# A diffusion-transformer layer with retention and attention: maxima transposed as float16 parts, value sums begun by their own products, one norm moved to VectorE

## The chip, the cores and the metric

The kernel runs on one core of one Trainium2 chip. The core has five engines that run side by side, each with its own queue of instructions in order: TensorE (PE, with its weight loads shown as PEld), VectorE (DVE), ScalarE (ACT), GpSimd (POOL) and SyncE (SP), which here issues the DMA transfers. Engines wait for one another through semaphores. TensorE writes to PSUM, a small memory of eight banks; the other data lies in SBUF. The metric is the device time of one execution in microseconds.

## The reference

One layer for a sequence of 2048 tokens with model width 1024, and a context of 256 tokens. Cut to what matters here:

```python
h = _modulate(_rmsnorm(x, norm1_g), sh1, sc1)
rq, rk, rv, rg, aq, ak, av = jnp.split(h @ w_in, SPLIT_IDX, axis=-1)
...
ret, _, _ = _bidir_retention(rq_h, rk_h, _heads(rv, RET_HEADS), log_gamma, s_f, s_b)
ret = _ret_out(ret, rg, ret_gn_g)
...
s = jnp.einsum('bqkgd,bskd->bkgqs', q, k).astype(jnp.float32) * ATT_SCALE
p = jax.nn.softmax(s, axis=-1).astype(v.dtype)
att = jnp.einsum('bkgqs,bskd->bqkgd', p, v)
...
x = x + g1 * (jnp.concatenate([ret, att], axis=-1) @ w_out)
h2 = _modulate(_rmsnorm(x, norm2_g), sh2, sc2)
x = x + g2 * _sqrelu_mlp(h2, w_ff1, w_ff2)
return _rmsnorm(x, final_norm_g)
```

Attention has 8 query heads of 64 channels on 2 key heads, over 2304 keys (2048 and the 256 of the context). All inputs are float32, and the kernel keeps about that precision by splitting operands into a high part and a remainder and multiplying the parts.

## The kernel before, in words

The kernel runs in three stretches. The first, to about 690 us, projects the input (`products`, L820) and stores queries, keys and the retention's operands to DRAM; its end also takes the row maxima of the first attention group. The second, to about 1640 us, is attention with the retention, the output projection and the second norm woven into it. The third is the feed-forward part.

**Steps and phases.** In the second stretch the order is written by hand. `on(k, phase, fn, ...)` (L988) files a call under a step number and a phase; the loop at L1643 walks the steps, and in each step the phases in the order begin, scores, piece, maximum, early, exp, cast, low, chain, pe, values, late, dma. Each engine executes its instructions in that program order. Besides, there is a list `chain` (L996) of small steps; `link` (L998) issues one of them after each of the phases maximum, low and late, and `settle` (L1002) issues from it until a named result is there.

**Attention.** A `Group` (L141) is one tile of 128 queries and one key head with its four query heads; there are 32 groups, and each takes NK = 18 steps, one for each tile of 128 keys. For group n:

- In steps 18n to 18n+17 `piece` (L160) multiplies queries by keys into a PSUM tile `mp` of 512 columns, and one step later `maximum` (L171, L178) reduces it on VectorE into `nm`. The tag `mp` has two buffers (`psS`, L956); the tile `st` of the scores has two of its own.
- In step 18n+18 `least` (L180) reduces `nm` to the negated row maximum of each head and writes it to columns 64 and 96 of `mt`, a float32 tile that is zero elsewhere but for a constant in column 80 (L974, L976). The two `mt` tiles serve the groups in turn.
- In the next step `turn` (L186) transposes the four heads of `mt` on TensorE into another `mp` tile. `rows` (L191) then copies partitions 64 to 127 of it to the second half of the query tile `qr` as float16, scaled by 1/8192, on ScalarE, and `rows2` (L194, L196), one step later in phase early, overwrites partitions 96 to 127 on VectorE with what float16 rounding left. So the negated maximum enters the scores as two extra rows of the contraction, multiplied by rows of `ks2` that hold 8192.
- From step 18n+22 on, `scores` (L198) makes one score tile per step with two products (L202, L203), `exp` (L205, L208) takes the exponential on ScalarE, `cast` (L210, L212) rounds two key tiles at once to float16 (`phi`), and `low` (L214) subtracts to get the remainder `plo`, on GpSimd for five of nine pairs of key tiles (L219) and on VectorE for the others (L221). Every second step `values` (L223) adds a pair of key tiles to the sums `o0` and `o1`, one PSUM bank each with two heads: for each key tile and head, `plo` times the 65 columns of values and ones (L235), then `phi` times 129 columns, values, ones and the values' remainders (L236). Before a group's first pair, a product of zeros with 258 columns for each bank (L227) clears the sums with the start flag.
- `evacuate`, `invert` and `combine` (L238 to L254) take the sums out and divide by the row sums.

**Output projection and second norm.** `output_tile` (L1248) does this for one tile of 128 tokens every 35 steps: transposes of the retention's and attention's result (L1259), products with `w_out` (L1274 to L1276), the residual sum into `y["x"]` (L1281, tile `xr`), its sum of squares, a store of it to DRAM (`store_x`, L1291), the root (`root`, through `chain`, two instructions on GpSimd, L1009 and L1010), the in-place multiplication by the root (`norm`, L1299, L1301, on GpSimd, three steps after the store is issued), and, for most tiles 3 and 4 steps later, its eight transposes on TensorE (`transpose_x`, L1306, four at a time), followed by `modulate` on VectorE (L1311) and `shift_` on GpSimd (L1316). For the last tile these transposes come from the list `rest`, between the first products of the feed-forward part.

**Feed-forward.** `up_part` (L1522 to L1524), `up_out` (L1542), `up_split` and `make_w2` (through `split16`, L70 and L71), `form_w1` (L1457) and `down` (L1582 to L1585) follow a loop over 32 blocks, with a few of the first block's instructions filed in the last steps of attention.

Of the kernel before, what the change touches and what calls it, by code (L numbers as in the profile page):

```python
# [11 lines left out]
F32 = mybir.dt.float32  # L12
F32R = mybir.dt.float32r
F16 = mybir.dt.float16
BF16 = mybir.dt.bfloat16
I32 = mybir.dt.int32
AF = mybir.ActivationFunctionType
ALU = mybir.AluOpType
AX = mybir.AxisListType
# [3 lines left out]
P = 128  # L23
# [6 lines left out]
NK = NT + NC  # L30
H = 4
CH = 128
HD = 64
# [3 lines left out]
PSHIFT = 8  # L37

ROW = 8192.0
VW = 2 * HD + 1  # L40
# [14 lines left out]
def layer_kernel(ctx: ExitStack, tc: tile.TileContext, a: dict, out: bass.AP):  # L55
    nc = tc.nc
    mm = nc.tensor.matmul

    const = ctx.enter_context(tc.tile_pool(name="const", bufs=1, reuse_waits="tile"))
    dram = ctx.enter_context(tc.tile_pool(name="dram", bufs=1, space=DRAM))  # L60

    ident = const.tile([P, P], F32, name="ident")
    make_identity(nc, ident)

    def split(hi, lo, src, eng=None):
        nc.scalar.activation(hi, src, AF.Copy)
# [74 lines left out]
    class Group:  # L141
# [36 lines left out]
            nc.vector.tensor_reduce(dst, src, axis=AX.X, op=ALU.max, negate=True)  # L178

        def least(self, mt):  # L180
            self.mt = mt
            nm = self.nm.rearrange("p a b c -> p (a b) c")
            for c in (64, 96):
                nc.vector.tensor_reduce(mt[:, :, c], nm, axis=AX.X, op=ALU.min)

        def turn(self):  # L186
            self.m = psS.tile([P, 4, P], F32, name="mp", tag="mp")
            for h in range(4):
                nc.tensor.transpose(self.m[:, h], self.mt[:, h], ident)

        def rows(self):  # L191
            nc.scalar.activation(self.qr[64:, 1], self.m[64:], AF.Copy, scale=1 / ROW)

        def rows2(self):  # L194
            lo = self.qr[96:, 1]
            nc.vector.scalar_tensor_tensor(lo, self.m[96:], 1 / ROW, lo, op0=ALU.mult, op1=ALU.subtract)  # L196

        def scores(self, kt):  # L198
            ps = self.s[kt] = psS.tile([P, 512], F32, name="st", tag="st")
# [23 lines left out]
        def values(self, j):  # L223
            if j == 0:
                self.o = [psV.tile([P, 2, VW], F32, name=f"o{b}", tag=f"o{b}") for b in range(2)]
                for o in self.o:
                    mm(o, zeros, wv[:, 0, :2, :VW], start=True, stop=False)  # L227
            hi, lo = self.hi.pop(j), self.lo.pop(j)
            for i in range(2):
                v = wv[:, self.g, 2 * j + i]  # L230
                for h in range(4):
                    o = self.o[h // 2][:, h % 2]
                    c = slice(h * P, (h + 1) * P)
                    last = 2 * j + i == NK - 1 and h % 2 == 1
                    mm(o[:, : HD + 1], lo[:, i, c], v[:, : HD + 1], start=False, stop=False)  # L235
                    mm(o, hi[:, i, c], v[:, :VW], start=False, stop=last)  # L236

        def evacuate(self):  # L238
            self.so = op.tile([P, 4, VW], F32, name="so", tag="so")
# [727 lines left out]
    nc.vector.tensor_tensor(unit, ident[:, 64:65], ident[:, 96:97], op=ALU.add)  # L967
    nc.vector.tensor_tensor(unit, unit, ident[:, 80:81], op=ALU.add)
    nc.vector.tensor_scalar_mul(unit, unit, ROW)
    zeros = vp.tile([P, P], F16, name="zeros")  # L970
    nc.vector.memset(zeros, 0.0)
    mts = [vp.tile([P, 4, P], F32, name=f"mt{i}") for i in range(2)]
    for mt in mts:
        nc.gpsimd.memset(mt, 0.0)  # L974

        nc.gpsimd.memset(mt[:, :, 80], PSHIFT * math.log(2.0) * HD**0.5)  # L976

    def more_keys(g, i):
        s = slice(i * 768, (i + 1) * 768)
# [8 lines left out]
    def on(k, phase, fn, *args):  # L988
        events.setdefault((k, phase), []).append((fn, args))
# [12 lines left out]
    def settle(what):  # L1002
        while what not in settled:
            link()
# [13 lines left out]
    def attention():  # L1018
        for n, g in enumerate(groups):
            k = NK * n  # L1020
# [5 lines left out]
                    on(k + i + 1, "maximum", g.maximum, i)  # L1026
            else:
                on(k + NK, "begin", g.load)
            on(k + NK, "chain", g.least, mts[n % 2])
            on(k + NK + 1, "piece", g.turn)  # L1030
            on(k + NK + 2, "cast", g.rows)
            on(k + NK + 3, "early", g.rows2)
            k += LAG
            for i in range(NK):
                on(k + i, "scores", g.scores, i)
# [212 lines left out]
    def output_tile(t, k, last):  # L1248
# [49 lines left out]

        def norm():  # L1299
            settle(("f", t))  # L1300
            nc.gpsimd.tensor_scalar(y["x"], y["x"], y["r"], 1.0, op0=ALU.mult, op1=ALU.mult)  # L1301

        def transpose_x(q):
            y["ps"] = bank(1)
# [503 lines left out]
```

## Time and profile before

| | us |
|---|---|
| median of 3 runs | 2947.15 (2943.18 to 2947.17) |
| the profiled execution | 2946.76 |
| its span, first to last instruction | 2945.0 |
| PE busy, share of the span | 2776.2, 94% |
| DVE busy | 2181.6, 74% |
| POOL busy | 1550.2, 53% |
| ACT busy | 1388.0, 47% |

The mean granted TensorE clock was 0.987 of full speed. In the page's groups, a line such as "L178 DVE TENSOR_REDUCE nm<-mp ... x576 | 390.9, 685 | 172.6 <-PE mp L165 143.3" reads: line 178 of the kernel, on VectorE, 576 instructions, 390.9 us busy, 685 ns each on average, 172.6 us of idle time of the engine just before them, 143.3 of it ended by TensorE's product at line 165. "x<-y" names the tile written and the tiles read. In a timeline a row has the start, the duration, the engine and the line, and in brackets the idle time before it with what ended it; instructions of one kind that follow each other are merged (x4). A matmul's recorded duration includes its way through the array, so those of neighbours overlap.

### The profile page before, as it was taken

The numbers are of one execution on the slowest core, as the hardware profiler recorded it, in microseconds if no ns is written. First come the engines' busy times: TensorE is split into PE (matmuls) and PEld (weight loads), VectorE is DVE, ScalarE is ACT, GpSimd is POOL, SyncE is SP. The second block draws the span as 40 slices with busy tenths as digits, with TensorE's granted clock in tenths as the row PEclk, the third lists the DMA queues.
The fourth block names the chain that finished last, engine by engine and source line by source line (L and its number), as shares of the span: only waits on it lengthen the run. The fifth ranks groups of instructions, "written<-read, shape, count | busy, mean of one in ns | idle before, by whom it ended". The sixth has DMA issues, their size and how long they took to land. (4 is left out here: it accounts for less than half of the span.)

```text
span 2945.0 us, 45295 instructions
## 1 busy us (share of the span) xinstructions
PE 2776.2 (94%) x17140; PEld 1648.8 (56%) x17140; DVE 2181.6 (74%) x3330; ACT 1388.0 (47%) x2280; POOL 1550.2 (53%) x1274
## 2 busy tenths in 40 slices
PE   7998898998799999999999899999999899999998
PEld 3777677775566666565666444444444344444443
DVE  5889847647987777777876577778777777777776
ACT  2333323325777777787777433333332333333332
POOL 3536326425876667887656656664443444444332
PEclk9999999999999999999999999999999999999999
DMA  9988843426412123332211723331114511111111
GB/s 300 340 283 280 271 154 107 160 67 201 137 46 81 49 63 121 90 104 85 73 63 51 273 92 101 104 102 60 53 51 154 173 60 47 54 51 51 58 44 58
DMA packets 265305, 346.95 MB, mean 118 GB/s; under 512 B 106231, under 2 KB 163831, under 8 KB 263294
## 3 DMA queue, kind: packets, MB, share of 16 engines
q1 hardware_dynamic: 254806, 336.57, 35.2%
q10 hardware_dynamic: 10280, 7.48, 0.9%
q8 instruction: 135, 2.21, 0.3%
q14 instruction: 84, 0.69, 0.1%
HBM read 272.52 MB, written 71.46 MB: 117 GB/s over the span
## 5 line engine op out<-in xcount | busy, mean ns | idle before, releaser
L178 DVE TENSOR_REDUCE nm<-mp 128x1 f32<-128x512 f32 (+1 forms) x576 | 390.9, 685 | 172.6 <-PE mp L165 143.3
L219 POOL TENSOR_TENSOR plo<-p,phi 128x1024 f16<-128x1024 f32 x160 | 353.7, 2212 | 172.9 <-ACT phi L212 139.6
L208 ACT ACTIVATE p<-st 128x512 f32<-128x512 f32 x576 | 338.1, 597 | 188.5 <-PE st L203 118.7
L1582 PE MATMUL pd<-w2hi,uhi 128*128 128x512 f16 x1024 | 388.0, 379 | 12.9 <-DVE acc L1585 12.6
L1583 PE MATMUL pd<-w2lo,uhi 128*128 128x512 f16 x1024 | 388.0, 379 | 0.6 <-DVE w2lo L71 0.6
L1584 PE MATMUL pd<-w2hi,ulo 128*128 128x512 f16 x1024 | 388.1, 379 | 0.0
L1585 DVE SCALAR_TENSOR_TENSOR acc<-pd,sc,acc 128x512 f32<-128x512 f32 x512 | 366.4, 739 | 5.7 <-PE pd L1584 5.6
L1522 PE MATMUL pu<-hf,w1f 128*128 128x512 f16 x896 | 340.1, 380 | 2.5 <-DVE q L1545 2.0
L1523 PE MATMUL pu<-hf,w1f 128*128 128x512 f16 x896 | 340.0, 379 | 0.0
L1524 PE MATMUL pu<-hf,w1f 128*128 128x512 f16 x896 | 339.8, 379 | 0.0
L824 PE MATMUL pso<-whi,hi_l 128*128 128x512 f32 (+1 forms) x768 | 295.8, 388 | 10.2 <-ACT xs L524 4.3
L212 ACT ACTIVATE phi<-p 128x1024 f16<-128x1024 f32 x288 | 303.8, 1055 | 0.0
L826 PE MATMUL pso<-whi,lo_l 128*128 128x512 f32 (+1 forms) x768 | 293.7, 383 | 4.1 <-DVE lo_l L67 4.1
L825 PE MATMUL pso<-wlo,hi_l 128*128 128x512 f32 (+1 forms) x768 | 292.9, 382 | 0.8 <-DVE wlo L67 0.7
L235 PE MATMUL o<-wv,plo 128*128 128x65 f16 x2304 | 235.9, 193 | 23.9 <-POOL plo L219 17.0
L221 DVE TENSOR_TENSOR plo<-p,phi 128x512 f16<-128x512 f32 x256 | 240.9, 942 | 18.6 <-ACT phi L212 15.7
L236 PE MATMUL o<-wv,phi 128*128 128x129 f16 x2304 | 243.8, 221 | 0.0
L235 PEld LDWEIGHTS <-plo 128*128 128x128 f16 x2304 | 206.7, 98 | 59.8 <-POOL plo L219 25.9
L202 PE MATMUL st<-qr,ks 128*128 128x512 f16 x576 | 220.2, 382 | 12.4 <-ACT p L208 10.4
L1534 POOL TENSOR_TENSOR r<-r 128x512 f32<-128x512 f32 x64 | 66.3, 1039 | 295.2 <-ACT r L1533 295.2
L203 PE MATMUL st<-qr,ks 128*128 128x512 f16 x576 | 220.0, 382 | 0.1
L165 PE MATMUL mp<-ks,qr 128*128 128x512 f16 x512 | 196.7, 384 | 23.0 <-DVE nm L178 22.2
(324 smaller groups left out, 5751.4 us busy)
## 6 DMA issues: line engine op xcount, KB each, us to landing
wm<-in_w_ff SPq DMA_DIRECT2D x64, 512.0 KB, 5.3
w1r<-in_w_ff SPq DMA_DIRECT2D x64, 512.0 KB, 4.6
ws<-in_w_ff SPq DMA_DIRECT2D x124, 256.0 KB, 3.5
wst<-in_w_in SPq DMA_DIRECT2D x60, 512.0 KB, 5.5
wst<-in_w_mod SPq DMA_DIRECT2D x32, 512.0 KB, 6.0
hf<-hp SPq DMA_DIRECT2D x56, 256.0 KB, 3.2
hf<-hf SPq DMA_DIRECT2D x14, 1024.0 KB, 7.1
orv<-rv SPq DMA_DIRECT2D x35, 256.0 KB, 4.0
```

Of the source, the lines that this page charges most:

```text
L178: nc.vector.tensor_reduce(dst, src, axis=AX.X, op=ALU.max, negate=True)
L208: nc.scalar.activation(self.p[kt // 2][:, kt % 2], self.s.pop(kt), AF.Exp, scale=HD**-0.5)
L212: nc.scalar.activation(hi, self.p[j], AF.Copy)
L219: nc.gpsimd.tensor_tensor(lo, p, hi, op=ALU.subtract)
L235: mm(o[:, : HD + 1], lo[:, i, c], v[:, : HD + 1], start=False, stop=False)
L1522: mm(pu[i], whi, hi, start=k == 0, stop=False)
L1523: mm(pu[i], whi, lo, start=False, stop=False)
L1524: mm(pu[i], wlo, hi, start=False, stop=k == 3)
L1582: mm(ps, uh, wh, start=f == 0, stop=False)
L1583: mm(ps, uh, wl, start=False, stop=False)
L1584: mm(ps, ul, wh, start=False, stop=f == NF - 1)
L1585: nc.vector.scalar_tensor_tensor(acc[:, c], ps, sc2, acc[:, c], op0=ALU.mult, op1=ALU.add)
```

## The change

Three edits in the attention stage, one of them in four functions.

The maxima: `least` now appends four small steps to `chain`: one reduction to a 128x4 float32 tile, a multiplication by 1/8192 into column 64 of `mt`, the same minus that column into column 96, and a mark that it is settled. It is filed in phase maximum of the step (begin for the first group) instead of chain. The `mt` tiles are float16, so that column 64 holds the rounded value and column 96 the remainder, and the constant in column 80 is divided by 8192 beforehand. `turn` first settles these steps and uses plain products with a float16 identity, `rows` copies without a scale, and `rows2` is gone.

The values: the products of zeros are gone. In `values` the product with `phi` comes before that with `plo`, and the first one of each bank carries the start flag.

The norm: the in-place multiplication of `y["x"]` by its root runs on VectorE instead of GpSimd, at the same place in the order.

```diff
+    ident16 = const.tile([P, P], F16, name="ident16")
+    nc.vector.tensor_copy(ident16, ident)
...
         def least(self, mt):
+
             self.mt = mt
+            m = sm.tile([P, 4], F32, name="least", tag="least")
             nm = self.nm.rearrange("p a b c -> p (a b) c")
-            for c in (64, 96):
-                nc.vector.tensor_reduce(mt[:, :, c], nm, axis=AX.X, op=ALU.min)
+            chain.append(lambda: nc.vector.tensor_reduce(m, nm, axis=AX.X, op=ALU.min))
+            chain.append(lambda: nc.vector.tensor_scalar_mul(mt[:, :, 64], m, 1 / ROW))
+            chain.append(
+                lambda: nc.vector.scalar_tensor_tensor(
+                    mt[:, :, 96], m, 1 / ROW, mt[:, :, 64], op0=ALU.mult, op1=ALU.subtract
+                )
+            )
+            chain.append(lambda: settled.add(("least", self.n)))
 
         def turn(self):
+            settle(("least", self.n))
             self.m = psS.tile([P, 4, P], F32, name="mp", tag="mp")
             for h in range(4):
-                nc.tensor.transpose(self.m[:, h], self.mt[:, h], ident)
+                mm(self.m[:, h], self.mt[:, h], ident16, start=True, stop=True)
 
         def rows(self):
-            nc.scalar.activation(self.qr[64:, 1], self.m[64:], AF.Copy, scale=1 / ROW)
-
-        def rows2(self):
-            lo = self.qr[96:, 1]
-            nc.vector.scalar_tensor_tensor(lo, self.m[96:], 1 / ROW, lo, op0=ALU.mult, op1=ALU.subtract)
+            nc.scalar.activation(self.qr[64:, 1], self.m[64:], AF.Copy)
...
                 self.o = [psV.tile([P, 2, VW], F32, name=f"o{b}", tag=f"o{b}") for b in range(2)]
-                for o in self.o:
-                    mm(o, zeros, wv[:, 0, :2, :VW], start=True, stop=False)
...
-                    mm(o[:, : HD + 1], lo[:, i, c], v[:, : HD + 1], start=False, stop=False)
-                    mm(o, hi[:, i, c], v[:, :VW], start=False, stop=last)
+
+                    mm(o, hi[:, i, c], v[:, :VW], start=j == i == h % 2 == 0, stop=False)
+                    mm(o[:, : HD + 1], lo[:, i, c], v[:, : HD + 1], start=False, stop=last)
...
-    zeros = vp.tile([P, P], F16, name="zeros")
-    nc.vector.memset(zeros, 0.0)
-    mts = [vp.tile([P, 4, P], F32, name=f"mt{i}") for i in range(2)]
+    mts = [vp.tile([P, 4, P], F16, name=f"mt{i}") for i in range(2)]
     for mt in mts:
         nc.gpsimd.memset(mt, 0.0)
 
-        nc.gpsimd.memset(mt[:, :, 80], PSHIFT * math.log(2.0) * HD**0.5)
+        nc.gpsimd.memset(mt[:, :, 80], PSHIFT * math.log(2.0) * HD**0.5 / ROW)
...
-            on(k + NK, "chain", g.least, mts[n % 2])
+            on(k + NK, "maximum" if n else "begin", g.least, mts[n % 2])
             on(k + NK + 1, "piece", g.turn)
             on(k + NK + 2, "cast", g.rows)
-            on(k + NK + 3, "early", g.rows2)
...
         def norm():
             settle(("f", t))
-            nc.gpsimd.tensor_scalar(y["x"], y["x"], y["r"], 1.0, op0=ALU.mult, op1=ALU.mult)
+            nc.vector.tensor_scalar_mul(y["x"], y["x"], y["r"])
```

## The prediction

> **What bounds the kernel now.** I read the page's strip of 40 slices for the stages, then the table by windows for their balance, then the waits of the stage that changes.
>
> ```profile
> 690.00:820.00 130.00, 105.01 (x1014) 74.14 (x1013) 117.73 (x218) 91.54 (x146) 99.04 (x67) 0.97 0.53 170
> 820.00:1640.00 820.00, 773.84 (x7226) 508.85 (x7224) 630.14 (x1105) 622.20 (x1019) 571.71 (x429) 1.00 0.25 78
> 1640.00:1720.00 80.00, 68.26 (x313) 31.20 (x312) 47.18 (x63) 26.55 (x49) 41.43 (x37) 0.98 0.72 265
> 1720.00:2945.00 1225.00, 1200.78 (x5552) 542.83 (x5549) 910.79 (x1182) 415.68 (x670) 551.49 (x421) 1.00 0.23 75
> ```
>
> Each row of the table by windows gives the stretch, its length, then the busy time of PE, PEld, DVE, ACT and POOL. The change touches attention (690 to 1640 us) and, through the norm, the hand-over to the feed-forward part (1640 to 1720). In the body of attention PE is busy 774 of 820 us, DVE 630, ACT 622, POOL 572: **TensorE sets the pace**, and the others have 20 to 30% in hand. The first 130 us are different: DVE is busy 118 of 130 and PE only 105. After 1720 nothing is changed and PE is busy 98%, so whatever is gained or lost before then arrives at the end unchanged.
>
> What PE waits for in 690 to 1640 (waiter, awaited, us in total, times, longest):
>
> ```profile
> DVE nm L178 <- PE mp L165: 119.2, 158, 2.0
> PEld L235 <- POOL plo L219: 25.9, 25, 3.0
> PE mp L165 <- DVE nm L178: 20.6, 34, 2.0
> PE o L235 <- POOL plo L219: 17.0, 13, 2.5
> PE o L235 <- DVE plo L221: 6.7, 14, 1.0
> PE bank L1306 <- POOL xr L1301: 3.5, 7, 1.1
> ```
>
> DVE waits for PE six times as long as PE for DVE, which fits a stage led by PE with short stalls. The groups that the change edits, over the whole span:
>
> ```profile
> L196 DVE SCALAR_TENSOR_TENSOR qr<-mp,qr 32x512 f16<-32x512 f32 x32 | 22.3, 697 | 4.8 <-ACT qr L192 3.8
> L1301 POOL TENSOR_SCALAR xr<-xr,cy_f 128x1024 f32<-128x1024 f32 x16 | 21.6, 1352 | 8.8 <-DMA x<-xr 8.8
> L227 PE MATMUL o<-wv,zeros 128*128 128x258 f16 x64 | 12.3, 274 | 0.0
> L184 DVE TENSOR_REDUCE mt<-nm 128x4 f32<-128x20 f32 x64 | 7.9, 165 | 0.0
> ```
>
> **1. TensorE work.** A matmul's recorded duration overlaps its neighbours, so I price by start to start, in a group without stalls:
>
> ```profile
> 834.48 0.60 PE L189 MATMUL mp<-ident,mt 128*128 128x128 f32 x4
> 834.92 0.38 PE L165 MATMUL mp<-ks,qr 128*128 128x512 f16 x1
> ...
> 849.60 0.39 PE L227 MATMUL o<-wv,zeros 128*128 128x258 f16 x2
> 849.82 0.19 PE L235 MATMUL o<-wv,plo 128*128 128x65 f16 x1
> 849.86 0.22 PE L236 MATMUL o<-wv,phi 128*128 128x129 f16 x1
> 849.91 0.19 PE L235 MATMUL o<-wv,plo 128*128 128x65 f16 x1
> ```
>
> The two zero products hold PE for 849.82 - 849.60 = 0.22 us per group; 32 groups: **7.0 us** go. Their row shows no idle time before them, so they hid no wait; should plo be late there, the cover of 0.22 us is lost, and the gain is smaller by that much. The four float32 transposes take 834.92 - 834.48 = 0.44 us. Float16 products of 128 columns are not in the trace; the nearest row is the 129-column float16 product, and a pair of 65 and 129 columns takes 0.09 us (849.82 to 849.91), so 128 columns take 128/194 of that, 0.06. Four: 0.24, a gain of 0.20 per group, **6.4 us** over 32. Ends: 0 (they cost what they did) to 7.7 (0.05 each). I take 6.4, since that row has the same type, nearly the same width and a weight load per product.
>
> The Trainium skill, "TensorE: Matmul & The Clock Gate", Back-to-back issue gap, gives about 81 ns per product for sustained pairs of weight load and 128-column matmul; by that the gain would be 32 x (0.44 - 0.32) = 3.8 us, an estimate from that page. The rows here speak against it: 0.09 us holds two such pairs.
>
> **2. High part first.** Each product of 129 columns now precedes the one that waits for plo. In the 27 waits of L235 (13 for POOL, 14 for DVE) PE has 0.06 us to do first: 1.6 us at most, I take **1.5**.
>
> **3. The maxima off VectorE.** The 32 instructions of L196 (22.3 us) go. The two reductions (L184, 0.165 us each) become one and two instructions on 128x4; I price those by L184 too, the nearest row with 128x4 out, so one such instruction more per group, +5.3 us in all. VectorE is relieved of 17.0 us here. ACT's copy (L192) keeps its size. Nothing on PE waits for L196, so its time counts only through what is queued behind it, and through the mp buffer that it holds. That buffer is worth a look:
>
> ```profile
> 742.80 0.25 DVE L184 TENSOR_REDUCE mt<-nm 128x4 f32<-128x20 f32 x2
> 744.08 0.68 DVE L178 TENSOR_REDUCE nm<-mp 128x1 f32<-128x512 f32 x1
> ...
> 743.19 0.63 PE L189 MATMUL mp<-ident,mt 128*128 128x128 f32 x4
> 744.81 0.38 PE L165 MATMUL mp<-ks,qr 128*128 128x512 f16 x1 [0.99 <-DVE nm L178]
> 747.86 0.38 PE L165 MATMUL mp<-ks,qr 128*128 128x512 f16 x1 [1.80 <-DVE nm L178]
> ...
> 744.15 0.59 ACT L192 ACTIVATE qr<-mp 64x512 f16<-64x512 f32 x1
> 749.00 0.70 DVE L196 SCALAR_TENSOR_TENSOR qr<-mp,qr 32x512 f16<-32x512 f32 x1
> ```
>
> Of two mp buffers one holds the transposed maxima from 743.19 until L196 ends at 749.70, and the next group's pieces share the other, each waiting for the reduction of the one before. After the change ACT's copy frees it at 744.74, three microseconds before the piece that waits until 747.86. Whether that piece gets it is decided when tiles are placed, which no row shows: 0 to all of the 20.6 us of that wait. I take **4**, near the low end, because the stalls I read are longest in the first 130 us, where DVE is full and a buffer alone does not help.
>
> The added wait: the transposes now need the third small instruction, issued behind the late phase of the step. Here that phase fills DVE from 743.05 to the next reduction at 744.08, so they could start about 744.2 instead of 743.19, with the next piece queued behind them on PE; but that piece waits for the reduction until 744.81 anyway. Cost 0 to 1.1 us in a group; where the late phase has nothing for DVE, none. I take **+0.5** in all.
>
> **4. The norm.** POOL loses 21.6 us. The seven attention waits of L1306 for it (**3.5 us**) go. POOL's plo tensors are no longer behind it: of 42.9 us (two views of the same stalls) I take **2**, between 0 and 6. VectorE gets 16 instructions, priced by the same shape and operation early in the program (minimum, median, maximum in ns):
>
> ```profile
> L416 DVE TENSOR_SCALAR x_l<-x_l,ry_x x16: 741/748/1230, 27.1 to 334.6; 128x1024 f32<-128x1024 f32 x16
> ```
>
> 16 x 0.75 = 12 us, so that VectorE's sum still falls by 5. They come in lumps, with the next reduction and so a piece on PE behind each. DVE's 158 waits for PE show slack that absorbs a lump within a few steps: I take 0.2 each, **+3**, between 0 and 16 x 1.23 = 20.
>
> **5. The hand-over.** The norm works in place, so it waits for the store of its tile. Twice that store is late, and then VectorE's queue stands, not POOL's:
>
> ```profile
> 1657.36 1.12 POOL L1301 TENSOR_SCALAR xr<-xr,cy_f 128x1024 f32<-128x1024 f32 x1 [3.74 <-DMA x<-xr]
> 1681.33 1.12 POOL L1301 TENSOR_SCALAR xr<-xr,cy_f 128x1024 f32<-128x1024 f32 x1 [5.06 <-DMA x<-xr]
> ...
> 1652.83 0.69 DVE L1266 TENSOR_TENSOR rl<-bank,rh 128x512 f16<-128x512 f32 x1
> 1676.47 0.68 DVE L1545 TENSOR_TENSOR r<-pu,w 128x512 f32<-128x512 f32 x1
> ...
> 1655.80 0.38 PE L1276 MATMUL bank<-wo,rl 128*128 128x512 f16 x1
> 1690.35 0.38 PE L1583 MATMUL pd<-w2lo,uhi 128*128 128x512 f16 x1 [0.61 <-DVE w2lo L71]
> ```
>
> At the first, rl (1652.83) is issued behind the norm and would start at 1657.36 + 0.75 = 1658.1; PE's 1655.80 product then starts near 1658.8, and the transposes, now at 1658.53, about 1.1 us later. At the second, everything of the first feed-forward block from 1676.47 on is behind the norm, so it starts at 1682.1; through r, ACT's relu and the splits, the w2lo that PE awaits at 1690.35 comes about 4 us later. Together **+5**, between +1 and the two waits whole, 8.8.
>
> **Sum.** -7.0 - 6.4 - 1.5 - 4 + 0.5 - 3.5 - 2 + 3 + 5 = -15.9. The profiled execution took 2946.8 us (span 2945.0), the median of the runs is 2947.15, so the sum applies to either: **2931 us**, forecast 2923 to 2940, chance 0.55.
>
> **Rivals.** *More comes free* (0.15): the freed buffer ends most of its stall (12 rather than 4), POOL's relief is worth 4, the norm's lumps and the hand-over cost 2 each: -7.0 - 6.4 - 1.5 - 12 - 3.5 - 4 + 4 = -30, **2917**. For it: DVE's and POOL's totals both fall. Against: the largest of these stalls lie where DVE is full.
>
> *The gain turns into another wait* (0.20): PE arrives earlier at products whose plo or p come no earlier. Half of the 13.4 us is lost, no buffer and no POOL relief is gained: -6.7 - 3.5 + 0.5 + 3 + 5 = -1.7, **2945**. For it: PE's waits for plo. Against: DVE and ACT are 20 to 25% idle.
>
> *The norm holds up VectorE* (0.10): each of 16 lumps reaches PE whole at L416's longest, 1.23 us, and both store waits count in full: 19.7 + 8.8 + 0.5 - 13.4 - 3.5 = +12, **2959**, slower. It decides from (13.4 + 3.5 - 8.8 - 0.5) / 16 = 0.48 us of PE time per norm. For it: L416's 1230 beside its median of 748. Against: in 14 of 16 tiles POOL's norm did not wait for the store. The Trainium skill, "SBUF — State Buffer", Who interferes with whom, has a rule that would bring this about: a VectorE instruction in a two-port mode and GpSimd lock each other out of a shared port for a whole instruction, and a scalar multiply from SBUF to SBUF is of that kind. L416's spread agrees with it; no row shows it at this place.
>
> That float16 transposes cost what float32 ones did would give 2937, inside the forecast.
>
> **Chances.** The measurement of this kernel can tell about 0.2% (6 us) from no change. Faster 0.69, the same 0.20, slower 0.11. The range 2914 to 2948 leaves out the end of the first rival, the upper end of the second, and the third.
>
> **What would show it.** No zero products; L189 float16 with 0.06 us between starts; L196 gone; DVE busy lower by 3 to 7 us, POOL by about 20; no wait of L1306 for POOL; in the hand-over DVE waiting for the store twice, 8 us together. Wrong if PE's waits on DVE or plo in 690 to 1640 grow by over 10 us, or if the stage is not shorter by about 20 us while the stretch 1640 to 1720 is longer by about 5.

## The result and the profile after

| | before | after |
|---|---|---|
| median | 2947.16 us (2943.18 to 2950.87, 4 runs) | 2988.12 us (2987.28 to 2988.95, 4 runs) |
| ratio to before | | 1.0139 [1.0122, 1.0157] |
| span of the profiled execution | 2945.0 us | 2986.7 us |
| mean granted clock | 0.987 | 0.981 |

The change made the kernel 41 us slower; 2931 was predicted, with 2914 to 2948 as its range. In the changed kernel the reduction to `least` is L187, the multiplication L188, the subtraction L190, the float16 transposes L200, the pieces L167, the maxima L180, the value products L241 (`phi`) and L242 (`plo`), VectorE's subtraction L228 and GpSimd's L226, the norm L1304 and its transposes L1309.

First the table by windows of the changed kernel, in the stretches used before (length, busy time of PE, PEld, DVE, ACT and POOL, granted clock, DMA):

```profile
690.00:820.00 130.00, 102.38 (x956) 72.09 (x955) 112.98 (x208) 85.22 (x136) 93.15 (x63) 0.92 0.51 164
820.00:1640.00 820.00, 749.41 (x6911) 487.09 (x6909) 652.32 (x1094) 604.59 (x990) 538.28 (x399) 0.98 0.24 72
1640.00:1720.00 80.00, 64.06 (x452) 36.82 (x450) 35.11 (x52) 32.35 (x60) 43.83 (x40) 0.94 0.62 226
```

In the body PE is busy 749 us where it was 774, and does fewer instructions (6911 for 7226) at a lower granted clock (0.98 for 1.00): it stands more. DVE is busy 652 for 630, though work was taken from it. The last score product of attention starts at 1662.0 us, at 1631.7 before: **30 of the 41 us are lost inside attention**, and 11 more between there and the tenth down product. After that the difference stays at 41.7.

The waits of PE in the changed kernel from 690 to 1670, where its attention ends:

```profile
PE mp L167 <- DVE nm L180: 27.0, 37, 2.5
PE mp L200 <- DVE mt L190: 22.0, 14, 3.5
PE o L242 <- POOL plo L226: 16.1, 15, 2.8
PE o L242 <- DVE plo L228: 8.2, 14, 1.2
```

The second line is new in size: the transposes wait 22 us for `mt`. The wait for the maxima has grown from 20.6 to 27.0 us, and that for `plo` (23.7 then, 24.3 now) has not moved, although the norm is gone from GpSimd's queue.

What VectorE's new instructions took, by their tile (minimum, median, maximum in ns, starts of the first and the last):

```profile
L187 DVE TENSOR_REDUCE least<-nm x32: 159/174/175, 659.4 to 1632.0; 128x4 f32<-128x20 f32 x32
L188 DVE TENSOR_SCALAR mt<-least x32: 161/172/2086, 659.7 to 1632.7; 128x4 f16<-128x4 f32 x32
L190 DVE SCALAR_TENSOR_TENSOR mt<-least,mt x32: 144/177/2092, 659.9 to 1632.9; 128x4 f16<-128x4 f32 x32
L1304 DVE TENSOR_SCALAR xr<-xr,cy_f x16: 752/1760/2616, 876.7 to 1717.9; 128x1024 f32<-128x1024 f32 x16
```

The reduction never exceeds 175 ns. The two others have the same size and nearly the same median, yet some of them last twelve times as long: 9 of the 32 of L188 and 7 of L190 are over 0.47 us. The norm, priced at 0.75 us, has that as its minimum and 1.76 as its median. The timelines of DVE and of POOL at two such places show what they stand for:

```profile
1418.96 0.17 DVE L187 TENSOR_REDUCE least<-nm 128x4 f32<-128x20 f32 x1
1420.32 2.09 DVE L188 TENSOR_SCALAR mt<-least 128x4 f16<-128x4 f32 x1
1422.44 0.18 DVE L190 SCALAR_TENSOR_TENSOR mt<-least,mt 128x4 f16<-128x4 f32 x1
...
876.67 2.62 DVE L1304 TENSOR_SCALAR xr<-xr,cy_f 128x1024 f32<-128x1024 f32 x1
```

```profile
1419.81 2.57 POOL L226 TENSOR_TENSOR plo<-p,phi 128x1024 f16<-128x1024 f32 x1
...
876.16 2.57 POOL L226 TENSOR_TENSOR plo<-p,phi 128x1024 f16<-128x1024 f32 x1
```

L188 writes four numbers per partition and ends at 1422.41, 0.03 us after GpSimd's subtraction (1419.81 + 2.57 = 1422.38), which had begun before it. The norm begins while GpSimd's instruction runs (to 878.73) and needs some 0.6 us after that. **A VectorE instruction of these kinds that begins beside a running GpSimd instruction stands until that one has ended.** The Trainium skill, "SBUF — State Buffer", Who interferes with whom, says that `tensor_scalar` in a two-port mode contends with GpSimd, that a VectorE instruction with two inputs in SBUF contends with a GpSimd instruction that reads SBUF, that whoever issues first holds the shared port and the other blocks, and that `tensor_reduce` on trn2 never contends. The four rows agree: the reduction takes 175 ns at most, the three others up to 2.1 and 2.6 us. In which mode L188 and L1304 run, no row shows.

The trace of before had a row that says the same, which the prediction did not read: VectorE's own subtraction, two inputs in SBUF, as a line of its tile.

```profile
L221 DVE TENSOR_TENSOR plo<-p,phi x256: 673/689/2635, 691.8 to 1635.1; 128x512 f16<-128x512 f32 x128
```

A median of 689 ns beside a maximum of 2635, in the stage that the change touches. In the trace of before, 81 of these 256 instructions take over 0.9 us; each of the 81 begins while a GpSimd instruction runs and ends 0.54 to 0.55 us after it.

The hand-over, in DVE's timeline and then in PE's, of the changed kernel:

```profile
1687.37 0.75 DVE L1304 TENSOR_SCALAR xr<-xr,cy_f 128x1024 f32<-128x1024 f32 x1 [4.31 <-DMA x<-xr]
1688.03 0.68 DVE L1269 TENSOR_TENSOR rl<-bank,rh 128x512 f16<-128x512 f32 x1
...
1717.93 0.75 DVE L1304 TENSOR_SCALAR xr<-xr,cy_f 128x1024 f32<-128x1024 f32 x1 [7.23 <-DMA x<-xr]
```

```profile
1688.77 1.12 PE L1262 MATMUL bank<-ident,ma 128*128 128x128 f32 x4 [5.21 <-DVE rl L1269]
...
1718.74 1.12 PE L1309 MATMUL bank<-ident,xr 128*128 128x128 f32 x4 [4.64 <-DVE xr L1304]
```

VectorE waits for the two late stores (11.5 us together), and PE stands 5.2 us behind `rl`, which is queued behind the first, and 4.6 us for the second norm itself.

### The profile page after: what moved, and what is told of

Same layout as the page of the kernel before. It is cut to its first block, busy times and chain, and to the rows that moved or that the text cites. A ratio compares the mean times of both kernels' runs of the same rounds, so it can differ in the third digit from the quotient of the medians.

```text
span 2986.7 us, 45103 instructions
## 1 busy us (share of the span) xinstructions
PE 2779.3 (93%) x17076; PEld 1644.9 (55%) x17076; DVE 2221.6 (74%) x3346; ACT 1388.8 (46%) x2280; POOL 1531.0 (51%) x1258
## 5 line engine op out<-in xcount | busy, mean ns | idle before, releaser
L180 DVE TENSOR_REDUCE nm<-mp 128x1 f32<-128x512 f32 (+1 forms) x576 | 389.9, 684 | 163.5 <-PE mp L167 138.7
L226 POOL TENSOR_TENSOR plo<-p,phi 128x1024 f16<-128x1024 f32 x160 | 354.9, 2219 | 184.2 <-ACT phi L219 151.6
L1585 PE MATMUL pd<-w2hi,uhi 128*128 128x512 f16 x1024 | 388.0, 379 | 15.3 <-DVE acc L1588 12.4
L228 DVE TENSOR_TENSOR plo<-p,phi 128x512 f16<-128x512 f32 x256 | 254.6, 996 | 22.8 <-ACT phi L219 22.2
L242 PE MATMUL o<-wv,plo 128*128 128x65 f16 x2304 | 237.5, 194 | 24.7 <-POOL plo L226 16.1
L241 PE MATMUL o<-wv,phi 128*128 128x129 f16 x2304 | 248.0, 222 | 0.0
L242 PEld LDWEIGHTS <-plo 128*128 128x128 f16 x2304 | 204.5, 99 | 56.1 <-POOL plo L226 21.8
L209 PE MATMUL st<-qr,ks 128*128 128x512 f16 x576 | 222.6, 386 | 12.7 <-ACT p L215 10.6
L241 PEld LDWEIGHTS <-phi 128*128 128x128 f16 x2304 | 210.3, 98 | 39.6 <-issue 18.5
L167 PE MATMUL mp<-ks,qr 128*128 128x512 f16 x512 | 199.8, 390 | 28.9 <-DVE nm L180 27.0
```

The costliest lines, as they stand in the source:

```text
L226: nc.gpsimd.tensor_tensor(lo, p, hi, op=ALU.subtract)
L241: mm(o, hi[:, i, c], v[:, :VW], start=j == i == h % 2 == 0, stop=False)
L1585: mm(ps, uh, wh, start=f == 0, stop=False)
```

## Experiments

All times are medians, all ratios are to runs of the kernel before on the same chip. Two theories stand behind the expectations: the **port** (instructions of the kinds above stand for GpSimd) and the **place** (the new work stands late in its step, or in lumps, whatever instructions it is made of).

### Each part alone

e1 takes only the hunks of `values` and `zeros`, e2 only those of the maxima, e3 only the line of the norm.

> The kernel before with the values' edit alone (no products of zeros, high part first). Both theories: the zero products held PE for 0.22 us in each of 32 groups, so 7 us go and nothing is added: about 2940 us, ratio 0.9975. Above 2947 would mean that the high-first order or the missing zero products cost something of their own.

> The kernel before with the maxima's edit alone. Theory 'shared port': the multiplication and the subtraction on 128x4 stand until a GpSimd instruction that runs at that time has ended; in the changed kernel that came to about 19 us on DVE (durations of 1.0 to 2.1 us instead of 0.17 in 16 of 64) and 22 us of PE waiting for mt, so 2955 to 2970 us and again about 16 long durations. Rival 'late in the step': the transposes wait because the third instruction is issued behind the late phase; then the durations would be short here, and the time about the same.

> The kernel before with the norm on VectorE alone. Theory 'shared port': each norm of the first 14 tiles takes 1 to 2.6 us instead of 0.75, about 15 us more on DVE in all, and the hand-over loses some 10 us because VectorE stands behind two late stores: 2960 to 2975 us. Rival (the prediction's price, 0.75 us each and 5 us at the hand-over, GpSimd relieved): 2945 to 2952 us.

| | us | ratio |
|---|---|---|
| e1, values | 2945.35 | 0.9993 [0.9981, 1.0004] |
| e2, maxima | 2969.73 | 1.0075 [1.0060, 1.0089] |
| e3, norm | 2970.88 | 1.0083 [1.0067, 1.0099] |

The three spans differ from 2945.0 by -4.6, +26.5 and +21.6 us, together +43.5 beside +41.7 of the whole change. The parts do not need one another to do harm: two of them cost over 20 us each. e2 and e3 came out where the port theory had them, with 18 of e2's 64 instructions of those kinds over 0.47 us. The values missed the expectation of 0.9975: they gain less than the 7 us of their zero products, no difference that can be measured here.

### The maxima: kind of instruction and place

e4 keeps e2's place, one link of the chain at a time, and computes the same two float16 parts by reductions alone (a maximum over one element is a copy, with a sign if wanted, and a sum over two is a difference). The 1/8192 stays in `rows`.

```diff
-            m = sm.tile([P, 4], F32, name="least", tag="least")
-            chain.append(lambda: nc.vector.tensor_reduce(m, nm, axis=AX.X, op=ALU.min))
-            chain.append(lambda: nc.vector.tensor_scalar_mul(mt[:, :, 64], m, 1 / ROW))
-            chain.append(
-                lambda: nc.vector.scalar_tensor_tensor(
-                    mt[:, :, 96], m, 1 / ROW, mt[:, :, 64], op0=ALU.mult, op1=ALU.subtract
-                )
-            )
+            m = sm.tile([P, 4, 2], F32, name="least", tag="least")
+            chain.append(lambda: nc.vector.tensor_reduce(m[:, :, 0], nm, axis=AX.X, op=ALU.min))
+            chain.append(lambda: nc.vector.tensor_reduce(mt[:, :, 64], m[:, :, :1], axis=AX.X, op=ALU.max))
+            chain.append(
+                lambda: nc.vector.tensor_reduce(m[:, :, 1], mt[:, :, 64:65], axis=AX.X, op=ALU.max, negate=True)
+            )
+
+            def low_part():
+                with nc.allow_low_precision(reason="the low part is meant to be float16"):
+                    nc.vector.tensor_reduce(mt[:, :, 96], m, axis=AX.X, op=ALU.add)
+
+            chain.append(low_part)
```

> The maxima's edit alone, but both parts made by reductions only (four of 128x4 in the same chain and phases, one more than in the change; the scale goes back to ScalarE's copy). A reduction has one input and one element out per row, so theory 'shared port' expects every one at 0.16 to 0.18 us, PE's wait for mt under 5 us and 2937 to 2943 us. Rival 'late in the step' expects the same waits as with the change's own instructions, 20 us or more, and a time like that of e2_maxima_alone.

2952.07 us, 1.0012 [1.0003, 1.0021]: most of the 1.0075 is gone with the kind of instruction, though not all, and the time stayed above the 2937 to 2943 us expected of the port alone. Every small reduction stayed short (176 ns at most), but PE still waited for `mt`, 9.8 us. Rows of e4's DVE timeline show a place where that wait arises:

```profile
745.66 0.17 DVE L187 TENSOR_REDUCE mt<-least 128x4 f16<-128x4 f32 x1
745.73 0.60 DVE L1108 SCALAR_TENSOR_TENSOR sf<-sf,cd,bank 128x128 f32<-128x128 f32 x2
746.24 2.21 DVE L1242 TENSOR_TENSOR wo<-wos,wo 128x512 f16<-128x512 f32 x1
748.37 0.14 DVE L189 TENSOR_REDUCE least<-mt 128x4 f32<-128x4 f16 x1
```

Between two links stands another instruction that itself stood for GpSimd (2.21 us; the shortest of its kind takes 0.67). So place may have a part. e5 and e6 are e2 and e4 with the small instructions issued directly, one behind the other, right after the last maximum:

```diff
-            chain.append(lambda: nc.vector.tensor_scalar_mul(mt[:, :, 64], m, 1 / ROW))
+            nc.vector.tensor_scalar_mul(mt[:, :, 64], m, 1 / ROW)
...
-            chain.append(lambda: settled.add(("least", self.n)))
+            settled.add(("least", self.n))
```

> The maxima's edit alone as in e2, but the three small VectorE instructions are issued one behind the other right after the last maximum, not one per link. Port theory (a tensor_scalar or scalar_tensor_tensor of VectorE with its data in SBUF stands until the GpSimd instruction that runs at that time has ended, wherever it is put): a quarter of the 64 stay long (1 to 2 us), the work before the first scores of a group keeps its price, and of the 22 us of e2 only the two early waits of TensorE for mt (2.6 and 3.2 us, where a 2.2 us product of wo and a locked subtraction stand between the links) go: 1.005 to 1.007 of before, 2962 to 2967 us. Place theory (the links are late in the step, other long instructions stand between them, and that is nearly all of the price): 0.999 to 1.002, 2945 to 2953 us, and TensorE waits under 8 us for mt (47 in e2).

> The maxima's edit alone by reductions as in e4, the four of them issued one behind the other right after the last maximum. Port theory with a remainder from the place: reductions of 0.16 us never stand, and issued at once (0.5 us in all) nothing stands between them: TensorE's wait for mt falls from 26 us (9.8 and 16.6) to under 6, the +5 us between 707 and 745 us of e4 goes, and the time is 0.997 to 0.9995 of before, 2939 to 2946 us. Rival (the remainder of e4 comes from the transposes as float16 products or from the wait that was added itself, wherever the reductions stand): as e4, 1.001, 2952 us.

| | one per link | at once |
|---|---|---|
| as in the change | e2: 1.0075 [1.0060, 1.0089] | e5: 1.0046 [1.0034, 1.0059] |
| by reductions | e4: 1.0012 [1.0003, 1.0021] | e6: 1.0023 [1.0013, 1.0033] |

e5 lies between the two theories: for these instructions the place is worth more than the port theory gave it, over a third of the price (1.0046 of 1.0075). PE's wait for `mt` fell from 19.2 us in e2 to 2.7 in e5, and still most of the price stayed. For the reductions, issuing them at once gained nothing. In e6 the wait for `mt` disappeared from PE's waits, as expected, but the time did not fall below before: this expectation failed. The waits went elsewhere, and one place shows how. First DVE's and POOL's timelines of before, then those of e6, at the same step (shifted by 2.3 us):

```profile
978.95 0.68 DVE L221 TENSOR_TENSOR plo<-p,phi 128x512 f16<-128x512 f32 x1
...
979.08 2.54 POOL L219 TENSOR_TENSOR plo<-p,phi 128x1024 f16<-128x1024 f32 x1 [3.59 <-DVE xr L1281]
```

```profile
977.28 2.15 DVE L229 TENSOR_TENSOR plo<-p,phi 128x512 f16<-128x512 f32 x1
...
976.76 2.13 POOL L227 TENSOR_TENSOR plo<-p,phi 128x1024 f16<-128x1024 f32 x1 [3.59 <-DVE nm L180]
```

Before, VectorE's subtraction began 0.13 us ahead of GpSimd's and ran through in 0.68, and GpSimd's took 2.54 where its median is 2.13. In e6 VectorE comes 0.65 us later within the step, mostly because four small reductions and not two are ahead of it, finds GpSimd 0.52 us under way, and stands for 1.5 us. PE's next piece waits 2.18 us there, the longest gap of these groups. So a delay of some tenths of a microsecond on VectorE's queue can change **which of the subtractions that were there already stand**. The total of that group, over the span, in before, e2, e6 and the changed kernel:

```profile
L221 DVE TENSOR_TENSOR plo<-p,phi 128x512 f16<-128x512 f32 x256 | 240.9, 942 | 18.6 <-ACT phi L212 15.7 <-POOL cy_f L1010 2.0 <-issue 0.3
```

```profile
L227 DVE TENSOR_TENSOR plo<-p,phi 128x512 f16<-128x512 f32 x256 | 256.3, 1002 | 22.6 <-ACT phi L218 22.1 <-issue 0.3 <-POOL cy_gn L1016 0.2
```

```profile
L229 DVE TENSOR_TENSOR plo<-p,phi 128x512 f16<-128x512 f32 x256 | 253.6, 992 | 21.0 <-ACT phi L220 20.7 <-issue 0.3
```

```profile
L228 DVE TENSOR_TENSOR plo<-p,phi 128x512 f16<-128x512 f32 x256 | 254.6, 996 | 22.8 <-ACT phi L219 22.2 <-issue 0.2 <-POOL cy_gn L1014 0.2
```

The same 256 instructions take 12 to 15 us longer in each of the three.

### The norm: queue and engine

e7 leaves the last two tiles, those of the hand-over, on GpSimd; e8 does so too and gives the other 14 to ScalarE.

```diff
-            nc.gpsimd.tensor_scalar(y["x"], y["x"], y["r"], 1.0, op0=ALU.mult, op1=ALU.mult)
+            if t < 2:
+                nc.gpsimd.tensor_scalar(y["x"], y["x"], y["r"], 1.0, op0=ALU.mult, op1=ALU.mult)
+            else:
+                nc.vector.tensor_scalar_mul(y["x"], y["x"], y["r"])
```

In e8 the last line is instead:

```diff
+                nc.scalar.activation(y["x"], y["x"], AF.Copy, scale=y["r"])
```

> The norm's edit alone as in e3, but the last two tiles (those of the hand-over behind attention) keep it on GpSimd. Theory: e3 paid about 11 us in attention (14 instructions that stand 0.15 to 1.9 us each for a GpSimd instruction, 12.6 us beyond 0.75 us each) and about 10 behind it (VectorE stands at the head of its queue for the store of x, and the products of the hand-over wait behind it): 1.003 to 1.005 of before, 2955 to 2961 us, and TensorE's wait of 5.4 us for rl at 1670 us is gone. Rival (the loss behind attention follows from what attention left late, or from the clock, not from the queue): as e3, 1.0075 to 1.009, 2969 to 2974 us.

> As e7, but the 14 norms run on ScalarE (activation Copy with the scale per row) in place of VectorE; the last two stay on GpSimd. Port theory: ScalarE's instruction does not stand for GpSimd's; it takes about 1.06 us (as 128x1024 on that engine elsewhere) 14 times, and no VectorE or GpSimd instruction is held up by it: 0.998 to 1.001 of before, 2941 to 2950 us. Lump theory (what costs is a 1 us instruction put ahead of short due work on an engine that feeds TensorE, whichever engine): about as e7, 1.003 to 1.005.

e7: 2959.88 us, 1.0041 [1.0027, 1.0055]. e8: 2950.73 us, 1.0010 [1.0002, 1.0019]. Both as the port theory had it, e8 at the upper edge. The hand-over is 10 us of e3's price: from the last score product to the last down product e3 loses 10.2 us and e7 1.1. The groups of the norm in e7 and e8:

```profile
L1304 DVE TENSOR_SCALAR xr<-xr,cy_f 128x1024 f32<-128x1024 f32 x14 | 23.6, 1684 | 2.9 <-DMA x<-xr 1.9 <-POOL cy_f L1010 0.9
```

```profile
L1304 ACT ACTIVATE xr<-xr,cy_f 128x1024 f32<-128x1024 f32 x14 | 16.1, 1150 | 1.8 <-POOL cy_f L1010 1.8
```

On VectorE the 14 take 23.6 us instead of 14 x 0.753 = 10.5, so they stand 13 us; on ScalarE, as a lump of 1.15 us each, they cost almost nothing. So a lump on ScalarE does not hurt as the one on VectorE does. Taking the norm from GpSimd gained nothing either, in e7 or e8.

### Idle instructions

In these two, the kernel before gets two instructions per group that nobody reads, right behind the two of `least`.

```diff
+            d = sm.tile([P, 4, 2], F32, name="dummy", tag="dummy")
+            for c in range(2):
+                nc.vector.tensor_reduce(d[:, :, c], nm, axis=AX.X, op=ALU.min)
```

In e10 the last line is instead:

```diff
+                nc.vector.tensor_scalar_mul(d[:, :, c], nm[:, :, c], 1 / ROW)
```

> The kernel before with two more reductions of nm per group (0.16 us each, about 10 us of VectorE in all) right behind the two of least, whose result nobody reads; transposes, values and norm as before. Collision theory (a few tenths of a us on VectorE's queue change which of its own later subtractions and products with data in SBUF begin beside a GpSimd instruction and stand for it; end to end the time grows by the growth of these stands, less the TensorE work removed: in e4 +13 and in e6 +11 us of stands against -6.4 us of transposes gave +6): 1.001 to 1.005 of before, 2950 to 2962 us, and the shift of the last scores is within 3 us of the growth of VectorE's stands (96 us before, duration beyond the shortest of its kind, 690 to 1650 us). Rival (the remainder of e4 and e6 comes from the transposes or the wait that was added): 0.9985 to 1.001, and no such agreement.

> As e9, but the two idle instructions per group are tensor_scalar of 128x4 from SBUF to SBUF. Theory: in place, count and size they are those of e9, but a quarter of the 64 stand 1 to 2 us for the GpSimd instruction beside them, 13 to 20 us in all: 1.005 to 1.010 of before, 2962 to 2977 us, with nobody waiting for their result. Rival (what costs is that TensorE waits for the result, mt): as e9.

e9: 2953.60 us, 1.0017 [1.0008, 1.0026]. e10: 2964.96 us, 1.0056 [1.0043, 1.0068]. Their groups, by the tile `dummy`:

```profile
L187 DVE TENSOR_REDUCE dummy<-nm x64: 156/162/169, 664.5 to 1612.4; 128x4 f32<-128x20 f32 x64
```

```profile
L187 DVE TENSOR_SCALAR dummy<-nm x64: 152/161/1935, 661.5 to 1621.0; 128x4 f32<-128x4 f32 x64
```

Both came out within the ranges expected of them; e9's interval still reaches that of its rival, which ends at 1.001, and fewer scalings stood than expected (11 of 64 are over 0.47 us, 10.8 us in all for 13 to 20). In e9, 23 of the 64 reductions begin beside a GpSimd instruction that goes on for at least 0.1 us, and none takes over 169 ns. Same place, same count, same size written, same median: the kind alone makes 11 us of difference, and 10.8 us is what the 64 scalings took beyond their median. Nothing uses their result, so a wait for the small instructions themselves is not needed for the loss. What e9 itself costs, two reductions of 0.16 us per group, has two readings that it can't separate: the 10.4 us that they add to VectorE, or the 6.3 us by which L221's group grew (247.2 for 240.9).

### A version that beats both

The maximum is only a shift of the scores, the same for every key of a row, and divides out of the softmax. So its low part can be left out. e11 does that: one reduction straight into float16, in the place of the two before, four float16 transposes, no `rows2`, no settle. e12 adds e1.

```diff
-            for c in (64, 96):
-                nc.vector.tensor_reduce(mt[:, :, c], nm, axis=AX.X, op=ALU.min)
+            with nc.allow_low_precision(reason="a shift of the scores, any value near the maximum"):
+                nc.vector.tensor_reduce(mt[:, :, 64], nm, axis=AX.X, op=ALU.min)
...
-                nc.tensor.transpose(self.m[:, h], self.mt[:, h], ident)
+                mm(self.m[:, h], self.mt[:, h], ident16, start=True, stop=True)
...
-            on(k + NK + 3, "early", g.rows2)
```

> A version that is meant to beat before: the maxima as one reduction straight into float16, in the place of the two; the low part of the maximum is left out (it is only a shift, the same for every key of a row, and divides out), so the subtraction on VectorE behind the transposes (0.70 us) goes as well; four float16 transposes, no instruction with two ports, no added settle. Collision theory: -6.4 us of TensorE work, VectorE has 0.86 us less per group, and its stands move by -5 to +5 us: 0.9965 to 1.000 of before, 2937 to 2947 us. Rival (the float16 transposes save nothing on the path): 1.000 to 1.003.

> e11 with the values' part of the change (no zero products). e1 gave 0.9993; the two parts touch different waits, so the sum: 2 to 4 us below e11, 0.995 to 0.9995 of before, 2933 to 2945 us. Rival (what TensorE gains is taken by its waits for the subtractions): as e11.

e11: 2936.80 us, **0.9963 [0.9950, 0.9975]**. e12: 2938.49 us, 0.9964 [0.9952, 0.9977]. Here float16 transposes come with a gain, once what feeds them does not stand; e11 also gives VectorE less to do. PE's wait for the maxima in e11, which was 20.6 us before:

```profile
PE mp L167 <- DVE nm L180: 14.8, 28, 1.8
```

The addition in e12 gave nothing in the end, so its rival came out and not the 2 to 4 us that were expected: its last score product is 4.7 us ahead of e11's, 2.8 of which it already had before attention, and in the hand-over the lead is lost. The tables by windows of e11 and of e12, at the second late norm (PE's busy time is the second number, the granted clock the third from the end):

```profile
1660.00:1680.00 20.00, 15.43 (x67) 6.92 (x66) 11.53 (x18) 10.19 (x20) 9.19 (x10) 0.91 0.77 289
```

```profile
1660.00:1680.00 20.00, 14.60 (x59) 6.62 (x58) 11.08 (x17) 9.64 (x18) 7.69 (x9) 0.83 0.82 290
```

PE stands more and is granted less: its waits for the two late norms on GpSimd are 2.2 and 4.8 us in e12 for 1.3 and 4.0 in e11. Whether the clock or the waits came first was not tried.

### The runs together

For each kernel: how much longer attention became (from the first reduction of maxima to the last score product, 1077.1 us before), beside a sum of three terms: the growth of VectorE's `plo` group (240.9 us before), what the part's own instructions took beyond their median or, for the norm, beyond 0.753 us, and the TensorE work that the prediction says is removed.

| kernel | `plo` group | own stands | TensorE | sum | attention |
|---|---|---|---|---|---|
| changed kernel | +13.7 | +33.7 | -13.4 | +34.0 | +31.8 |
| e1 | +3.8 | 0 | -7.0 | -3.2 | -2.5 |
| e2 | +15.4 | +19.1 | -6.4 | +28.1 | +23.7 |
| e3 | +1.6 | +12.6 | 0 | +14.2 | +11.7 |
| e4 | +8.7 | 0 | -6.4 | +2.3 | +5.4 |
| e5 | +6.1 | +13.6 | -6.4 | +13.3 | +11.9 |
| e6 | +12.7 | 0 | -6.4 | +6.3 | +7.4 |
| e7 | +2.9 | +13.0 | 0 | +15.9 | +11.0 |
| e8 | +0.1 | 0 | 0 | +0.1 | +3.1 |
| e9 | +6.3 | 0 | 0 | +6.3 | +6.1 |
| e10 | +8.7 | +10.8 | 0 | +19.5 | +17.6 |
| e11 | +6.6 | 0 | -6.4 | +0.2 | -10.5 |
| e12 | +9.8 | 0 | -13.4 | -3.6 | -12.4 |

Eleven of the thirteen agree within 5 us, though PE is busy 93% of attention before. But the sum has no term for TensorE's clock, and in the changed kernel that is not small. The table by windows for attention and for the stretch from there to the tenth down product, first before, then the changed kernel:

```profile
554.60:1631.70 1077.10, 999.94 (x8734) 677.17 (x8733) 809.03 (x1430) 748.62 (x1214) 697.10 (x520) 0.99 0.29 92
1631.70:1689.40 57.70, 50.17 (x282) 25.95 (x281) 26.79 (x45) 21.87 (x42) 32.29 (x33) 0.97 0.84 319
```

```profile
553.10:1662.00 1108.90, 1001.27 (x8670) 674.11 (x8669) 847.21 (x1443) 749.03 (x1214) 682.33 (x506) 0.97 0.29 89
1662.00:1731.00 69.00, 54.01 (x281) 27.08 (x280) 28.47 (x46) 21.59 (x42) 30.01 (x31) 0.90 0.73 274
```

PE should be busy 13.4 us less in attention and is busy 1.3 us more; the other 30.5 us of the 31.8 are time in which it stands. The trace has what goes with it: in stretches of 3.4 to 10.2 us the granted clock is half of full speed (a 512-column float16 product takes 0.63 us in one of them, at 1689.68 in the changed kernel, for 0.38 otherwise), and in attention these stretches withhold 30.7 us of full speed, for 11.9 before. So VectorE's stands of 47.4 us arrive as 30.5 us of waiting, and the lower clock took about what the removed TensorE work was worth; that the sum of the changed kernel fits so well is in part luck. Eleven of the twelve half-speed stretches there begin during a wait of PE of over 1.2 us or within 1 us after it, so they go with the waits; no run varies the clock alone. The loss does not need them: e5, e7 and e10 lose 11 to 18 us in attention, and what the clock withholds there is within 1.7 us of before.

The last two kernels gain 9 to 11 us more than the sum. The clock withholds 5.1 us less there in e11 and 6.8 in e12, and VectorE has 22.3 + 7.9 - 5.5 = 24.7 us less plain work in total; these two were not separated. The sum is a description, not a law. That the growth of the `plo` group causes its share of the time, rather than goes along with it, is shown at single places such as 977 us and not by a run that removes it alone.

## Why the prediction was wrong, by its steps

**What bounds the kernel.** "TensorE sets the pace, and the others have 20 to 30% in hand" was read from busy sums, and the busy time of DVE includes its stands. The slack is an average; a piece two buffers deep and a `plo` due two steps later see the single delay.

**1. TensorE work.** Right for the transposes, instruction by instruction. In the changed kernel's timeline of PE four float16 transposes hold it 0.22 us (0.24 predicted):

```profile
866.82 0.39 PE L200 MATMUL mp<-ident,mt 128*128 128x128 f16 x4
867.04 0.38 PE L167 MATMUL mp<-ks,qr 128*128 128x512 f16 x1
```

That is 0.055 us each, nearer to the row of the trace than to the 81 ns of the Trainium skill ("TensorE: Matmul & The Clock Gate", Back-to-back issue gap), from which the prediction's other estimate came. But PE's busy time in attention did not fall by the predicted 13.4 us: it rose by 1.3, at the lower granted clock, for which the sum had no term. And less TensorE work is only worth its size if nothing else becomes late: e1 got 2.5 of its 7.0 us in attention, and PE's wait for `p` there rose from 10.4 to 14.3 us. This is the second rival, in part.

**2. High part first.** The 1.5 us are not visible: PE's waits for `plo` are 24.3 us for 23.7.

**3. The maxima off VectorE.** This step failed, and it is the larger of two failures. "I price those by L184 too, the nearest row with 128x4 out" chose a row by its shape, though the small reductions stood in none of these runs. The two instructions that it stood for took 19.0 us more than their medians (31 of each from 690 to 1670, means of 483 and 479 ns for medians of 172 and 177), the links between them let other stands in (e2 to e5: 1.0075 to 1.0046), and PE's wait for `mt`, of which "+0.5 in all" was to be added, was 22.0 us for 1.5 before. The buffer of "4" ended nothing here, since the wait for the maxima rose from 20.6 to 27.0; e11, without the small instructions, shows it at 14.8, but there VectorE has less to do as well, and the two were not separated.

**4. The norm.** The third rival had the mechanism and the right place, and was given 0.10; the forecast priced the norm at "0.75" and "0.2 each". The 14 in attention took 25.3 us, 14.7 beyond 0.753 each, and in e3 attention became longer by 11.7 us, 0.84 per norm: past the 0.48 us from which that rival decides. PE's waits for GpSimd's norm in attention are gone as predicted, but 3.1 us of waits for `modulate` on VectorE took their place, and the relief of GpSimd's queue, "2", did not come.

**5. The hand-over.** Right in mechanism, short in size: "+5, between +1 and 8.8", measured 11.3 in the changed kernel (41.7 - 30.4) and 10.2 in e3, and 1.1 in e7, where VectorE's queue does not wait. The first norm starts as long after the last score product as before (25.4 us for 25.7), the second 6.3 us later (55.9 for 49.6), and that one is itself on PE's path, 4.6 us. Of the 11.3 us, 3.8 are longer busy time of PE, at a granted clock of 0.90 for 0.97.

The sum said -15.9. It put the stands of VectorE's new instructions at nothing for the small ones, by the price of a reduction, and at 0.2 us for a norm, and it had no term for the growth of the old ones. They came to +47 in attention, and PE stood 30.5 us longer there; the lower clock used up the -13.4 of TensorE's work, and the hand-over cost 11 instead of 5.

The signs named beforehand for being wrong both came: PE's waits on DVE grew by more than 10 us, those for `mt` alone by 20.5, and the stage became longer. DVE's busy time rose by 40 us (2221.6 for 2181.6) where a fall of 3 to 7 was expected.

## What to carry to other kernels

Before an instruction is moved to VectorE or added to it, read minimum, median and maximum of the groups beside it, by kind and not by shape: where a group with its data in SBUF shows a maximum far above its median, find the GpSimd instruction beside the longest one, and price the new instruction with such stands. On average a stand cost each new instruction 0.17 us (e10), 0.31 us (the two small ones of the change) and 1.05 us (the norm); the most was what GpSimd's instruction beside it had left. Small copies and sums on VectorE can be written as small reductions, which stood in none of these runs, and a larger scaling was given to ScalarE (e8); neither beat the kernel before. The edit that did was the one that removed the instructions (e11). An engine's queue should not take over an in-place step that waits for a late store unless everything queued behind it can wait as long.

## What was not expected of the hardware

- The smallest instruction stands as long as a large one: 128x4 from SBUF to SBUF, 0.17 us by itself, took up to 2.09 us beside GpSimd's subtraction of 2.1 to 2.6 us.
- The one that begins first wins, so a few tenths of a microsecond decided between 0.68 us and 2.15 us of the same instruction at the same step, and reductions that do not stand may cost time by shifting others (e9, though its plain work may be the cause).
- The granted clock fell with the stalls: 0.92 in 690 to 820 us after the change for 0.97 before, and 0.83 in one stretch of e12. In the changed kernel's attention PE is busy about 15 us longer than the removed work would have it (+1.3 for -13.4), an estimate of what the clock cost there; no run changed the clock by itself.
